# One matmul of a threshold guess later, the order in branch b's mixing, and other costs in a planner that interleaves a top-k search with dense work

## The chip, the cores and the metric

The kernel runs on one core of one Trainium2 chip. The metric is the device time of one execution in microseconds (us): 4260.66 before, the median of 3 runs from 4255.64 to 4262.76. Engines are written as in the profile: PE is TensorE's matmul, PEld its weight load, DVE is VectorE, ACT is ScalarE, POOL is GpSimd, SP is SyncE, which issues the DMAs.

## The reference

One encoder block over 4096 tokens of width 1024. Cut to what matters here:

```python
h = rms_norm(x, norm_g)
q, k, v, qi, ki, wi, z_a, u_b, z_b, gates = jnp.split(h @ w_in, SPLIT_POINTS, axis=-1)
# sparse attention, blocks of 128 queries: 8 index heads of 32 score all keys, the best 256 are kept
logits = jnp.einsum('bqhd,bsd->bqhs', qib, ki)
iscore = jnp.einsum('bqhs,bqh->bqs', jax.nn.relu(logits), wib)
iscore = jnp.where(allowed[None], iscore, -jnp.inf)      # allowed: by chunks of 64 tokens, not later
_, idx = lax.top_k(iscore, 256)                          # then softmax attention over these keys
a = dsa_attention(...) * silu(z_a)
# branch b, four groups of 128 channels, windows 2, 4, 8, 16: trailing mean minus the token, a 128x128 map
pooled = (c - lagged) / count - u_b
b = einsum('bsgc,gcd->bsgd', pooled, pool_w) * pool_scale * silu(z_b)
g = sigmoid(gates + merge_bias)
out = x + (g[0] * (a @ w_branch_a) + g[1] * (b @ w_branch_b)) @ w_out
```

## The kernel before

The kernel runs in stages. The first projects q, k, v and the index part and stores them in HBM, to about 445 us of the profile. The stage that the change touches, `phase_index`, runs from there to about 2100 us. Then a flag is checked (`phase_exact`, whose exact path is entered only where a threshold search did not settle), and attention and the output projections follow. Only the second stage's order differs between the two kernels.

In that stage two kinds of work lie beside each other:

- **Scoring and search.** For a block of 128 queries, each of 8 index heads and each piece of up to 1024 keys is one scoring tile, 624 in all: matmuls (L769) into one of 2 PSUM buffers `ps`, a Relu on ScalarE into one of 4 buffers `rl` (L772), and a multiply-accumulate on VectorE (L774) into an SBUF area of scores, `ring`. When a group of blocks is scored, its threshold is searched in 7 rounds: sign passes on ScalarE that count the scores above the threshold (L859), and small VectorE steps (L811 to L847); then the best are picked (`finish`).
- **Dense work.** The columns u, z_b, z_a and the gates of `h @ w_in`, in f32 made of three matmuls each (weight high · h high, weight high · h low, weight low · h high; L1056 to L1058). 24 matmuls make a unit of 128 columns x 256 tokens in one of 3 PSUM buffers `pd`; a unit is planned in `DU` = 4 quarters. A gate's unit is read out by a sigmoid (L1004, or L997 for z_a, which VectorE then multiplies, L999) and stored.

Branch b (`pool` in `dense`) takes the units of u and z_b, makes the windowed sums on GpSimd (L971), subtracts the token on VectorE (L980), rounds the result to its high part `ph` on ScalarE (L982), makes the low part `pl` on GpSimd (L983), and mixes channels by three matmuls through `mm3` (L347 high·`ph`, L348 high·`pl`, L349 low·`ph`). VectorE then scales and stores (L987).

The search starts from a guess of all thresholds (`guess`): a VectorE reduce and memset (L611, L612), a 128x1 matmul that sums over partitions (L639), a square root on ScalarE (L641), six VectorE steps (L615 to L620), another square root (L643) and some fifteen VectorE steps (L623 to L637). Its scratch lies at the end of `ring`. The second group's scores and every search wait for it.

The order on every engine is written by a planner before the program is built. Each step has an engine, a cost in us, a key (due time) and the steps it comes after. `Plan.run` is a list scheduler: at each time it gives a free engine the step with the lowest key whose inputs are done and whose buffers are free; a result reaches another engine `lat` later (here `LAT` = 0.1 us), a DMA's 2.0 us. On the chip each engine works its list strictly in order and waits at each instruction for its inputs, so a step that is listed too early blocks all behind it. The keys of scoring run from `t0[i]` to `t0[i+1]`, whose distance `span(i)` is `STR` times an estimate of the most loaded engine; those of dense units rise by 2.6 per unit; branch b's and the gates' read-outs are far ahead of all (`DEV`). Costs are constants in the code.

Of the kernel before, what the change touches and what calls it, by code (L numbers as in the profile page):

```python
# [12 lines left out]
F32 = mybir.dt.float32  # L13
# [4 lines left out]
AF = mybir.ActivationFunctionType  # L18
OP = mybir.AluOpType
# [4 lines left out]
S, D, P = 4096, 1024, 128  # L24
# [17 lines left out]
LAT = 0.1  # L42
# [28 lines left out]
DU = 4  # L71
# [11 lines left out]
CHN = 4.0  # L83
RING = 9984
T_IN = 10.0
STR = 0.8
PRL = 30.0
TKL = 30.0
DEV = 10000.0
# [157 lines left out]
class K:  # L247
# [338 lines left out]
    def guess(self, pl, new, ring, key):  # L586

        nc = self.nc
# [13 lines left out]
        ks, ones, c = take(1), take(P), take(1)  # L602
        a1, a2, a3 = take(*sh), take(*sh), take(*sh)
        mu, sd, sk, t = (take(NB) for _ in range(4))
# [3 lines left out]
        pc = new("pd")  # L608
# [27 lines left out]
            v.tensor_tensor(t, t, sd, op=OP.mult)  # L636
            v.tensor_tensor(self.SL, t, ch, op=OP.mult)  # L637
        s = pl.add("dve", 0.5, key, first, self.index_done)
        s = pl.add("pe", 0.1, key, lambda: nc.tensor.matmul(pc.t[:, 0:1], ones, ks, start=True, stop=True), [s], [pc])  # L639
        s = pl.add("dve", 0.2, key, lambda: v.tensor_copy(c, pc.t[:, 0:1]), [s], [pc])  # L640
        s = pl.add("act", 1.7, key, lambda: nc.scalar.activation(a1, self.qn2[:, :, 0:8], AF.Sqrt, scale=c), [s])  # L641
        s = pl.add("dve", 2.0, key, powers, [s])
# [3 lines left out]
    def phase_index(self):  # L646
# [13 lines left out]
        pl = Plan()  # L660
        new = pl.new
        w2 = 2 * P
# [81 lines left out]
        def scores(b, key, total, free):  # L744
# [6 lines left out]
            while os_:  # L751
# [8 lines left out]
                for h in range(8):  # L760
                    for o in some:
                        n = min(1024, L - o)
                        k_ = key(1)
                        ps, rl = new("ps"), new("rl")

                        def mm(ps=ps, o=o, n=n, h=h):
                            for s in range(0, n, 512):
                                e = min(n, s + 512)
                                pe.matmul(ps.t[:, s:e], t.t[:, h], self.kis[:, o + s:o + e], start=True, stop=True)  # L769
                        m = pl.add("pe", n * 0.42e-3, k_, mm, have + [base[o]] + ([s5] if o + n > S - P else []),  # L770
                                   use=[ps, t])
                        r = pl.add("act", 0.05 + n * 0.834e-3, k_, lambda ps=ps, rl=rl, n=n: act.activation(  # L772
                            rl.t[:, :n], ps.t[:, :n], AF.Relu), [m], use=[ps, rl])
                        prev[o] = pl.add("dve", 0.1 + n * 1.04e-3, k_, lambda rl=rl, o=o, n=n, h=h: v.scalar_tensor_tensor(  # L774
                            acc[:, o:o + n], rl.t[:, :n], self.wi[:, b, h:h + 1], acc[:, o:o + n], op0=OP.mult,
                            op1=OP.add), [r, prev[o], s2], use=[rl])
# [148 lines left out]
            ends.append(topk(i, t0[i + 1] - TKL, scored))  # L925

        self.dense(pl, new, rp)
        pl.run(LAT)
        es.close()
        self.esr.close()  # L930
        self.phase_exact()
# [2 lines left out]
    def dense(self, pl, new, rp):  # L934
# [19 lines left out]
        def pool(c, g, t, pu, pz, done):  # L954
# [11 lines left out]
            def sums():  # L966
# [6 lines left out]
                if c == 0:  # L973
# [5 lines left out]
            ph, pq, pm = new("ph"), new("pl"), new("pd")  # L979
            s = pl.add("dve", 0.4, k, lambda: v.scalar_tensor_tensor(  # L980
                cur.t[:, 16:], cur.t[:, 16:], 1.0 / win, u.t[:, 16:], op0=OP.mult, op1=OP.subtract), [s], use=[cur, u])
            s = pl.add("act", 0.31, k, lambda: act.activation(ph.t, cur.t[:, 16:], AF.Copy), [s], use=[cur, ph])  # L982
            s = pl.add("pool", 0.69, k, lambda: po.tensor_tensor(pq.t, cur.t[:, 16:], ph.t.bitcast(F32), op=OP.subtract),  # L983
                       [s], use=[cur, ph, pq])
            s = pl.add("pe", 0.33, k, lambda: self.mm3(pm.t[:, :w2], lambda k: wm[g][0], lambda k: wm[g][1],
                                                       lambda k: ph.t, lambda k: pq.t, 1), [s], use=[ph, pq, pm])
            s = pl.add("dve", 0.4, k, lambda: v.scalar_tensor_tensor(  # L987
                zs.t, pm.t[:, :w2], self.col[:, 24 + g:25 + g], zs.t, op0=OP.mult, op1=OP.mult), [s, m], use=[pm, zs])
            pl.add("dma", 0.4, k, lambda: dma(self.bD[g, :, c * w2:(c + 1) * w2], zs.t), [s], use=[zs])
# [41 lines left out]
        for s, mine in enumerate(sweeps):  # L1031
# [3 lines left out]
            for c in range(S // w2):  # L1035
# [12 lines left out]
                for m, (kind, i) in enumerate(mine):  # L1048
                    pd = new("pd")
                    wh, wl, have = W[s, m]  # L1050
                    for half in range(DU):
                        def mm(half=half, pd=pd, wh=wh, wl=wl, H=H):
                            out = pd.t[:, :w2].rearrange("p (r n) -> p r n", n=P)
                            for k in range(KT // DU * half, KT // DU * (half + 1)):
# [1 line left out]
                                pe.matmul(out, wh.t[:, k], r1, start=(k == 0), stop=False)  # L1056
                                pe.matmul(out, wh.t[:, k], r2, start=False, stop=False)  # L1057
                                pe.matmul(out, wl.t[:, k], r1, start=False, stop=(k == KT - 1))  # L1058
                        prev = pl.add("pe", 2.58 / DU, t, mm, lds + [have, prev], use=[pd, wh, wl] + H)
                        t += unit / DU  # L1060
                    if kind == "u":
                        pu = (pd, prev)
# [586 lines left out]
```

## Time and profile before

| | us |
|---|---|
| median of 3 runs | 4260.66 (4255.64 to 4262.76) |
| the profiled execution | 4263.0 |
| its span, first to last instruction | 4261.2 |
| PE busy | 4142.3 (97%) |
| DVE busy | 3218.5 (76%) |
| ACT busy | 2340.6 (55%) |
| POOL busy | 1900.7 (45%) |

The span is 1.8 us shorter than the time of the same execution. The mean granted TensorE clock is 0.986 of full speed. A wait is read as "engine, line <- who ended it": the idle time of the engine just before that line's instruction. A window gives the busy time of each engine in a stretch. Times of the stretches count from the span's start.

### The profile page before, as it was taken

The page shows a single profiled execution, that of the slowest core. Times are in us where ns is not written, and L with a number is a line of the kernel's source. Part 1 is how long each engine was busy: PE and PEld are TensorE (multiplying, and loading weights), DVE is VectorE, ACT ScalarE, POOL GpSimd, SP SyncE. Part 2 cuts the span into 40 slices and gives each one's busy share as a digit, 9 for nine tenths or more (in the row PEclk, how much of TensorE's full clock was granted, in tenths as well). Part 3 has the DMA queues.
Part 4 walks back from the last instruction along what each step waited for, and adds up shares of the span by engine and source line. Part 5 has one row for each costly group of instructions (what it writes and reads, how often), then busy time and mean ns, then how long its engine had stood idle before and what let it go on. Part 6 is the DMA issues. An engine that isn't in the chain of part 4 may idle for free.

```text
span 4261.2 us, 76795 instructions
## 1 busy us (share of the span) xinstructions
PE 4142.3 (97%) x27746; PEld 3496.7 (82%) x27747; DVE 3218.5 (76%) x7786; ACT 2340.6 (55%) x3977; POOL 1900.7 (45%) x1717
## 2 busy tenths in 40 slices
PE   8999899999999999999799999999999999999999
PEld 7888899899999998999756666666666658999998
DVE  6555688889889888788679999999999995434342
ACT  4444588777877877887455555555555552111110
POOL 3445322323234333010047888888999991111110
PEclk9999999999999999999889999999999999999999
DMA  6666644545445446566543212212111116544442
GB/s 225 236 243 231 218 160 167 172 172 187 162 174 168 160 170 196 201 234 206 184 84 72 58 45 49 47 48 52 43 41 38 23 42 190 163 134 151 137 144 77
DMA packets 446651, 586.34 MB, mean 138 GB/s; under 512 B 149373, under 2 KB 342457, under 8 KB 442042
## 3 DMA queue, kind: packets, MB, share of 16 engines
q1 hardware_dynamic: 446266, 581.39, 41.9%
q8 instruction: 219, 3.59, 0.3%
q14 instruction: 166, 1.36, 0.1%
HBM read 388.54 MB, written 175.54 MB: 132 GB/s over the span
## 4 chain that ended last, share of the span: by engine, by line
PE 57%; DVE 2%; DMA 1%; issue 1%; ACT 0%; POOL 0%; SPq 0%; DVEq 0%; ACTq 0%; POOLq 0%
PE pv L1339 11%; PE st L1323 7%; PE ps L1284 6%; PE st L1324 5%; PE pd L1056 3%; PE pd L1057 3%; PE pd L1058 3%; PE po L1537 3%; PE po L1538 3%; PE po L1539 3%; PE pa L1538 3%; PE pa L1539 3%; PE pa L1537 3%; PE ps L769 1%; PE st L1375 1%; PE st L341 1%
## 5 line engine op out<-in xcount | busy, mean ns | idle before, releaser
L1056 PE MATMUL pd<-h,wgh 128*128 128x256 f32 x3584 | 1018.6, 284 | 1.3 <-DVE zsm L976 1.3
L1057 PE MATMUL pd<-h,wgh 128*128 128x256 f32 x3584 | 1012.0, 282 | 0.0
L1058 PE MATMUL pd<-h,wgl 128*128 128x256 f32 x3584 | 1011.4, 282 | 0.0
L1354 POOL TENSOR_TENSOR acc<-acc,tt 128x1024 f32<-128x1024 f32 x388 | 927.5, 2391 | 103.0 <-ACT tt L1330 80.7
L1330 ACT ACTIVATE tt<-tt 128x512 f32<-128x512 f32 x1056 | 652.7, 631 | 556.0 <-DVE tt L1327 553.9
L1327 DVE TENSOR_TENSOR tt<-st,bT 128x512 f32<-128x512 f32 x1056 | 693.6, 684 | 76.4 <-PE st L1324 59.3
L774 DVE SCALAR_TENSOR_TENSOR ring<-rl,wi,ring 128x1024 f32<-128x1024 f32 (+7 forms) x624 | 689.8, 1148 | 12.9 <-ACT rl L772 10.3
L1056 PEld LDWEIGHTS pd<-h,wgh 128*128 128x128 f32 x3584 | 680.3, 190 | 19.6 <-issue 1.5
L1057 PEld LDWEIGHTS pd<-h,wgh 128*128 128x128 f32 x3584 | 681.2, 190 | 14.6
L1290 DVE CUSTOM_DVE_ANT_0 jk<-ps,bias 128x1024 bf16<-128x1024 f32 (+7 forms) x640 | 656.2, 1029 | 47.2 <-PE ps L1284 46.0
L1058 PEld LDWEIGHTS pd<-h,wgl 128*128 128x128 f32 x3584 | 681.4, 190 | 0.0
L772 ACT ACTIVATE rl<-ps 128x1024 f32<-128x1024 f32 (+7 forms) x624 | 539.0, 889 | 133.8 <-PE ps L769 61.4
L1339 PE MATMUL pv<-tt,vv 128*64 128x256 f32 x4224 | 525.0, 389 | 0.0
L859 ACT ACTIVATE sg<-ring,tk 128x2048 fp8e4<-128x2048 f32 (+7 forms) x322 | 485.4, 1509 | 38.3 <-DVE tk L846 21.2
L1323 PE MATMUL st<-qa,kk 128*128 128x512 f32 x1056 | 453.2, 429 | 10.5 <-ACT sm L1379 5.5
L1339 PEld LDWEIGHTS pv<-tt,vv 128*64 128x64 f32 x4224 | 279.6, 137 | 210.3 <-issue 71.6
L1324 PE MATMUL st<-qm,kl 65*128 65x512 f32 x1056 | 420.9, 399 | 2.3 <-DMA qm<-maxD 2.3
L1579 POOL TENSOR_TENSOR ga<-ga,gb 128x256 f32<-128x256 f32 x128 | 100.3, 792 | 617.4 <-DVE ga L1574 504.2
L1284 PE MATMUL ps<-kk,qa 128*128 128x512 f32 (+3 forms) x1152 | 362.2, 390 | 0.7 <-DVE mx L1290 0.7
L769 PE MATMUL ps<-kis,qT 128*128 128x512 f32 (+3 forms) x1136 | 334.9, 382 | 14.7 <-ACT rl L772 14.4
L1502 ACT ACTIVATE yh<-ga 128x256 fp32r<-128x256 f32 x128 | 53.3, 418 | 500.7 <-PE po L1538 297.8
L1323 PEld LDWEIGHTS st<-qa,kk 128*128 128x128 f32 x1056 | 200.1, 190 | 153.5 <-DVE tt L1327 49.2
(331 smaller groups left out, 7801.9 us busy)
## 6 DMA issues: line engine op xcount, KB each, us to landing
h<-hD SPq DMA_DIRECT2D x192, 1024.0 KB
hlD<-rhl SPq DMA_DIRECT2D x32, 1216.0 KB
gD<-sgm SPq DMA_DIRECT2D x256, 128.0 KB
x<-x SPq DMA_DIRECT2D x32, 512.0 KB
wraw<-w_in SPq DMA_DIRECT2D x32, 512.0 KB
hD<-hh SPq DMA_DIRECT2D x32, 512.0 KB
hD<-hl SPq DMA_DIRECT2D x32, 512.0 KB
q<-hlD SPq DMA_DIRECT2D x32, 512.0 KB
```

The costliest lines, as they stand in the source:

```text
L774: prev[o] = pl.add("dve", 0.1 + n * 1.04e-3, k_, lambda rl=rl, o=o, n=n, h=h: v.scalar_tensor_tensor(acc[:, o:o + n], rl.t[:, :n], self.wi ...
L1056: pe.matmul(out, wh.t[:, k], r1, start=(k == 0), stop=False)
L1057: pe.matmul(out, wh.t[:, k], r2, start=False, stop=False)
L1058: pe.matmul(out, wl.t[:, k], r1, start=False, stop=(k == KT - 1))
L1284: pe.matmul(ps.t[:, s:e], Q[b][0].t[:, 4 * g + j], kk[:, g, o + s:o + e], start=True, stop=True)
L1290: v.tensor_tensor_reduce(out=jk.t[:, :n], in0=ps.t[:, :n], in1=BI[b][0].t[:, o:o + n], scale=1.0, scalar=-3e38, op0=OP.add, op1=OP.max, ac ...
L1323: pe.matmul(s.t, kk[:, g, o], qa.t[:, hs], start=True, stop=False)
L1324: pe.matmul(s.t, kl[:, g, o], qm.t[:, hs], start=False, stop=True)
L1327: ad = pl.add("dve", 0.602, i, lambda s=s, tt=tt, r=r, kt=kt: v.tensor_tensor(tt.t[:, r], s.t, bc(bt.t[:, kt:kt + 1], [P, 4, P]), op=OP.ad ...
L1330: E[kt] = pl.add("act", 0.52, i, lambda tt=tt, r=r: act.activation(tt.t[:, r], tt.t[:, r], AF.Exp), [ad], use=[tt])
L1339: pe.matmul(pv.t[64 * f:64 * f + 64], vv[:, k, 64 * g:64 * g + 64], T[k // 2].t[:, k % 2, 2 * f:2 * f + 2], start=(k == 0), stop=(k == b))
L1354: gp.tensor_tensor(acc.t, first, tt.t, op=OP.add)
```

## The change

Two due times and several costs change, a matmul's place in the plan, and the order of three matmuls:

- `STR`, which stretches the due times of scoring, goes from 0.8 to 0.85.
- The guess's 128x1 matmul gets the key 25 instead of -40.
- The planner's cost of scoring matmuls goes from 0.42 to 0.45 ns an element, of a dense unit from 2.58 to 2.86 us, of branch b's rounding from 0.31 to 0.42, its low part from 0.69 to 1.0, its mixing from 0.33 to 0.36, and `run` gets twice the latency, 0.2 us.
- Branch b's mixing runs high·`ph`, low·`ph`, high·`pl`, so that the low part `pl` is read by the third matmul instead of the second.

```diff
--- before.py
+++ after.py
@@ -83,7 +83,7 @@
 CHN = 4.0
 RING = 9984
 T_IN = 10.0
-STR = 0.8
+STR = 0.85
 PRL = 30.0
 TKL = 30.0
 DEV = 10000.0
@@ -636,7 +636,7 @@
             v.tensor_tensor(t, t, sd, op=OP.mult)
             v.tensor_tensor(self.SL, t, ch, op=OP.mult)
         s = pl.add("dve", 0.5, key, first, self.index_done)
-        s = pl.add("pe", 0.1, key, lambda: nc.tensor.matmul(pc.t[:, 0:1], ones, ks, start=True, stop=True), [s], [pc])
+        s = pl.add("pe", 0.1, 25, lambda: nc.tensor.matmul(pc.t[:, 0:1], ones, ks, start=True, stop=True), [s], [pc])
         s = pl.add("dve", 0.2, key, lambda: v.tensor_copy(c, pc.t[:, 0:1]), [s], [pc])
         s = pl.add("act", 1.7, key, lambda: nc.scalar.activation(a1, self.qn2[:, :, 0:8], AF.Sqrt, scale=c), [s])
         s = pl.add("dve", 2.0, key, powers, [s])
@@ -767,7 +767,7 @@
                             for s in range(0, n, 512):
                                 e = min(n, s + 512)
                                 pe.matmul(ps.t[:, s:e], t.t[:, h], self.kis[:, o + s:o + e], start=True, stop=True)
-                        m = pl.add("pe", n * 0.42e-3, k_, mm, have + [base[o]] + ([s5] if o + n > S - P else []),
+                        m = pl.add("pe", n * 0.45e-3, k_, mm, have + [base[o]] + ([s5] if o + n > S - P else []),
                                    use=[ps, t])
                         r = pl.add("act", 0.05 + n * 0.834e-3, k_, lambda ps=ps, rl=rl, n=n: act.activation(
                             rl.t[:, :n], ps.t[:, :n], AF.Relu), [m], use=[ps, rl])
@@ -925,7 +925,7 @@
             ends.append(topk(i, t0[i + 1] - TKL, scored))
 
         self.dense(pl, new, rp)
-        pl.run(LAT)
+        pl.run(2 * LAT)
         es.close()
         self.esr.close()
         self.phase_exact()
@@ -979,11 +979,14 @@
             ph, pq, pm = new("ph"), new("pl"), new("pd")
             s = pl.add("dve", 0.4, k, lambda: v.scalar_tensor_tensor(
                 cur.t[:, 16:], cur.t[:, 16:], 1.0 / win, u.t[:, 16:], op0=OP.mult, op1=OP.subtract), [s], use=[cur, u])
-            s = pl.add("act", 0.31, k, lambda: act.activation(ph.t, cur.t[:, 16:], AF.Copy), [s], use=[cur, ph])
-            s = pl.add("pool", 0.69, k, lambda: po.tensor_tensor(pq.t, cur.t[:, 16:], ph.t.bitcast(F32), op=OP.subtract),
+            s = pl.add("act", 0.42, k, lambda: act.activation(ph.t, cur.t[:, 16:], AF.Copy), [s], use=[cur, ph])
+            s = pl.add("pool", 1.0, k, lambda: po.tensor_tensor(pq.t, cur.t[:, 16:], ph.t.bitcast(F32), op=OP.subtract),
                        [s], use=[cur, ph, pq])
-            s = pl.add("pe", 0.33, k, lambda: self.mm3(pm.t[:, :w2], lambda k: wm[g][0], lambda k: wm[g][1],
-                                                       lambda k: ph.t, lambda k: pq.t, 1), [s], use=[ph, pq, pm])
+
+            def mix():
+                for i, (x, y) in enumerate(((0, ph), (1, ph), (0, pq))):
+                    pe.matmul(pm.t[:, :w2], wm[g][x], y.t, start=(i == 0), stop=(i == 2))
+            s = pl.add("pe", 0.36, k, mix, [s], use=[ph, pq, pm])
             s = pl.add("dve", 0.4, k, lambda: v.scalar_tensor_tensor(
                 zs.t, pm.t[:, :w2], self.col[:, 24 + g:25 + g], zs.t, op0=OP.mult, op1=OP.mult), [s, m], use=[pm, zs])
             pl.add("dma", 0.4, k, lambda: dma(self.bD[g, :, c * w2:(c + 1) * w2], zs.t), [s], use=[zs])
@@ -1056,7 +1059,7 @@
                                 pe.matmul(out, wh.t[:, k], r1, start=(k == 0), stop=False)
                                 pe.matmul(out, wh.t[:, k], r2, start=False, stop=False)
                                 pe.matmul(out, wl.t[:, k], r1, start=False, stop=(k == KT - 1))
-                        prev = pl.add("pe", 2.58 / DU, t, mm, lds + [have, prev], use=[pd, wh, wl] + H)
+                        prev = pl.add("pe", 2.86 / DU, t, mm, lds + [have, prev], use=[pd, wh, wl] + H)
                         t += unit / DU
                     if kind == "u":
                         pu = (pd, prev)
```

No tile, buffer count or shape changes. From about L986 on a line of the kernel before has a number 3 higher in the changed one (dense matmuls L1059 to L1061, z_a's sigmoid L1000, gates L1007); the mixing matmuls stand in L988.

The planned order moves at many places; three are shown. On TensorE, at the stage's start, the kernel before has these rows (`pd` is the dense unit's PSUM tile or the guess's, `pt` the PSUM tile of the transposes of `qi`, the index queries of a block):

```order
L1056 MATMUL pd_5395<-h_5020,wgh_5032 128x256
L1057 MATMUL pd_5395<-h_5022,wgh_5032 128x256
L1058 MATMUL pd_5395<-h_5020,wgl_5033 128x256
L639 MATMUL pd_5420<-ring 128x1
L341 MATMUL pt_5422<-identr,qi_5384 128x128 x4
L1056 MATMUL pd_5395<-h_5020,wgh_5032 128x256
L1057 MATMUL pd_5395<-h_5022,wgh_5032 128x256
L1058 MATMUL pd_5395<-h_5020,wgl_5033 128x256
L1056 MATMUL pd_5395<-h_5020,wgh_5032 128x256
```

And the changed kernel, at the same place:

```order
L1059 MATMUL pd_5396<-h_5020,wgh_5032 128x256
L1060 MATMUL pd_5396<-h_5022,wgh_5032 128x256
L1061 MATMUL pd_5396<-h_5020,wgl_5033 128x256
L341 MATMUL pt_5420<-identr,qi_5384 128x128 x4
L1059 MATMUL pd_5396<-h_5020,wgh_5032 128x256
L1060 MATMUL pd_5396<-h_5022,wgh_5032 128x256
L1061 MATMUL pd_5396<-h_5020,wgl_5033 128x256
L1059 MATMUL pd_5396<-h_5020,wgh_5032 128x256
```

The guess's matmul is gone from here, and the transposes of `qi` come right behind the dense matmuls; it now stands 217 rows later, between two quarters of a dense unit.

On ScalarE, around the guess, the kernel before has (`u` and `sgm` are branch b's and the gates' read-outs, `ring` the guess's scratch; ACT_TABLE_LOAD loads a function table):

```order
L641 ACTIVATE ring<-qn_75,ring 128x256
L961 ACTIVATE u_5361<-pd_5363 128x256
L962 ACT_TABLE_LOAD
L962 ACTIVATE sgm_5464<-pd_5395 128x256
L740 ACTIVATE qT_5423<-pt_5437 128x512
L1004 ACTIVATE sgm_5491<-pd_5445,col 128x256
L643 ACT_TABLE_LOAD
L643 ACTIVATE ring<-ring 128x32
L982 ACTIVATE ph_5531<-s_5480 128x256
L1004 ACT_TABLE_LOAD
L1004 ACTIVATE sgm_5550<-pd_5484,col 128x256
```

The changed kernel, whose first table load in the stage comes earlier, under L962, has there:

```order
L772 ACTIVATE rl_5793<-ps_5783 128x1024
L772 ACTIVATE rl_5805<-ps_5795 128x1024
L641 ACT_TABLE_LOAD
L641 ACTIVATE ring<-qn_75,ring 128x256
L1007 ACT_TABLE_LOAD
L1007 ACTIVATE sgm_5839<-pd_5773,col 128x256
L772 ACTIVATE rl_5847<-ps_5819 128x1024
L772 ACTIVATE rl_5861<-ps_5830 128x1024
L643 ACT_TABLE_LOAD
L643 ACTIVATE ring<-ring 128x32
L772 ACTIVATE rl_5874<-ps_5866 128x1024
L772 ACTIVATE rl_5898<-ps_5870 128x1024
```

The two square roots now stand among the scoring's Relus (L772) and each is followed by a sigmoid with its own table load: five loads in the stage instead of three.

ScalarE's last rows of the stage, before (`sg` is a sign pass over `ring`, `tk` the thresholds; L997 is the sigmoid of a z_a unit):

```order
L997 ACTIVATE sgm_27851<-pd_27779 128x256
L859 ACTIVATE sg_27874,tk_26462<-ring,tk_26462 128x384
L997 ACTIVATE sgm_27884<-pd_27843 128x256
L859 ACTIVATE sg_27892,tk_26462<-ring,tk_26462 128x512
L997 ACTIVATE sgm_27944<-pd_27876 128x256
L859 ACTIVATE sg_27960,tk_26462<-ring,tk_26462 128x384
L859 ACTIVATE sg_27969,tk_26462<-ring,tk_26462 128x512
L997 ACTIVATE sgm_27971<-pd_27937 128x256
L859 ACTIVATE sg_28003,tk_26462<-ring,tk_26462 128x384
L859 ACTIVATE sg_28006,tk_26462<-ring,tk_26462 128x512
L859 ACTIVATE sg_28034,tk_26462<-ring,tk_26462 128x384
L859 ACTIVATE sg_28042,tk_26462<-ring,tk_26462 128x512
```

In the changed kernel, the last sign pass and what comes behind it:

```order
L859 ACTIVATE sg_27320,tk_25572<-ring,tk_25572 128x384
L1000 ACTIVATE sgm_27329<-pd_27291 128x256
L859 ACTIVATE sg_27360,tk_25572<-ring,tk_25572 128x512
L1000 ACTIVATE sgm_27375<-pd_27322 128x256
L1000 ACTIVATE sgm_27421<-pd_27368 128x256
L1000 ACTIVATE sgm_27456<-pd_27408 128x256
L1000 ACTIVATE sgm_27485<-pd_27447 128x256
L1000 ACTIVATE sgm_27517<-pd_27478 128x256
```

Behind its last sign pass stand 23 read-outs of z_a units, the last rows of the stage on ScalarE; in the kernel before the search's sign passes come last.

On TensorE, a mixing of branch b, before:

```order
L1057 MATMUL pd_6018<-h_5685,wgh_5168 128x256
L1058 MATMUL pd_6018<-h_5630,wgl_5169 128x256
L347 MATMUL pd_6028<-ph_6008,wm0h 128x256
L348 MATMUL pd_6028<-pl_6015,wm0h 128x256
L349 MATMUL pd_6028<-ph_6008,wm0l 128x256
L769 MATMUL ps_6032<-kis,qT_5423 128x512 x2
L1056 MATMUL pd_6018<-h_5630,wgh_5168 128x256
L1057 MATMUL pd_6018<-h_5685,wgh_5168 128x256
```

And in the changed kernel:

```order
L1060 MATMUL pd_6038<-h_5622,wgh_5322 128x256
L1061 MATMUL pd_6038<-h_5567,wgl_5323 128x256
L988 MATMUL pd_6048<-ph_6002,wm0h 128x256
L988 MATMUL pd_6048<-ph_6002,wm0l 128x256
L988 MATMUL pd_6048<-pl_6029,wm0h 128x256
L769 MATMUL ps_6055<-kis,qT_5421 128x512 x2
L1059 MATMUL pd_6038<-h_5567,wgh_5322 128x256
L1060 MATMUL pd_6038<-h_5622,wgh_5322 128x256
```

The low part `pl` is read by the third of the three. In the order as a whole, 9948 of the stage's 10752 dense matmuls stand ahead of the 601st scoring tile before and 9300 in the changed kernel.

## Rows read from the trace of the kernel before

**Rows 1.** Page, part 1: busy us of each engine (share of the span) xinstructions
```profile
PE 4142.3 (97%) x27746; PEld 3496.7 (82%) x27747; DVE 3218.5 (76%) x7786; ACT 2340.6 (55%) x3977; POOL 1900.7 (45%) x1717
```

**Rows 2.** Waits of PE, 440 to 2101 us: us in total, times, longest
```profile
PE ps L769 <- ACT rl L772: 14.4, 10, 4.3
PE pd L639 <- DVE ring L612: 14.2, 1, 14.2
PE pc L1078 <- DVE one L1076: 12.7, 1, 12.7
PE pd L348 <- POOL pl L983: 11.2, 17, 1.3
PE pd L347 <- ACT ph L982: 2.2, 3, 1.6
PE pd L347 <- ACT sgm L1004: 1.4, 1, 1.4
```

**Rows 3.** Windows: us, busy of PE, PEld, DVE, ACT, POOL (x), clock, DMA
```profile
490.00:1988.00 1498.00, 1466.15 (x11292) 1408.47 (x11291) 1282.40 (x3787) 1166.38 (x1697) 385.02 (x441) 1.00 0.52 179
583.00:710.00 127.00, 127.00 (x986) 122.81 (x985) 109.56 (x283) 93.30 (x128) 28.81 (x36) 1.00 0.48 173
847.00:1030.00 183.00, 181.60 (x1409) 175.30 (x1408) 160.53 (x503) 138.61 (x203) 45.50 (x59) 1.00 0.46 163
1030.00:1103.00 73.00, 68.27 (x520) 64.41 (x520) 66.47 (x215) 57.52 (x82) 33.18 (x33) 1.00 0.59 197
1225.00:1376.00 151.00, 145.33 (x1111) 139.19 (x1111) 138.49 (x460) 112.92 (x168) 60.65 (x67) 0.99 0.51 176
2030.00:2088.00 58.00, 57.49 (x484) 57.28 (x482) 41.41 (x226) 28.68 (x65) 0.00 (x0) 1.00 0.60 211
```

**Rows 4.** Timeline of PE, 449 to 466 us: start, duration, [idle before <-releaser]
```profile
449.87 0.28 PE L1058 MATMUL pd<-h,wgl 128*128 128x256 f32 x1
464.31 0.56 PE L639 MATMUL pd<-ring 128*128 128x1 f32 x2 [14.16 <-DVE ring L612]
465.20 0.72 PE L341 MATMUL pt<-identr,qi 128*128 128x128 f32 x4 [0.33 <-DMA qi<-hlD]
```

**Rows 5.** Timeline of SyncE's queue, 457 to 463 us
```profile
461.56 0.38 SPq L729 DMA_DIRECT2D qi<-hlD  x1
```

**Rows 6.** Lines of ACT, 460 to 480 us: busy, mean ns | idle before
```profile
L643 ACT ACT_TABLE_LOAD x1 | 1.3, 1283 | 0.0
```

**Rows 7.** Windows of the guess's two VectorE blocks, columns as in rows 3
```profile
466.99:469.64 2.65, 2.65 (x15) 2.65 (x15) 2.58 (x7) 2.39 (x4) 1.29 (x3) 0.50 1.02 416
474.43:479.24 4.81, 4.81 (x40) 4.56 (x39) 4.33 (x16) 3.87 (x6) 3.54 (x4) 1.00 0.96 286
```

**Rows 8.** Line 983 on POOL: ns min/median/max, and who waited (us, times)
```profile
L983 POOL TENSOR_TENSOR pl<-s,ph x64: 721/1008/1874, 474.8 to 1645.2; 128x256 fp32r<-128x256 f32 x64
  PE pd L348: 11.2, 17
```

**Rows 9.** Waits of PE in 1030:1103 (first two), then 1225:1376 us
```profile
PE ps L769 <- ACT rl L772: 1.6, 2, 1.4
PE pd L1056 <- DVE zsm L976: 1.3, 1, 1.3
PE ps L769 <- ACT rl L772: 1.8, 2, 1.6
```

**Rows 10.** Timelines of PE, ACT and DVE, 2087 to 2101 us
```profile
2087.21 0.28 PE L1058 MATMUL pd<-h,wgl 128*128 128x256 f32 x1
2100.15 0.27 PE L1078 MATMUL pc<-flag,one 128*1 128x32 f32 x2 [12.66 <-DVE one L1076]
2087.52 0.38 ACT L997 ACTIVATE sgm<-pd 128x256 f32<-128x256 f32 x1 [0.25 <-PE pd L1058]
2090.08 0.42 DVE L999 TENSOR_TENSOR zsm<-pd,sgm 128x256 f32<-128x256 f32 x1
```

## The prediction

> **What bounds the kernel now.** I read the engine table first. TensorE is busy 97% of a 4261.2 us span [rows 1], so the kernel gets shorter only where TensorE idles; an engine that gets faster beside it gives nothing. The profiled execution took 4263.0 us (span plus 1.8 us around it), 2.3 us above the median of the runs, 4260.66. I add up against 4263.0 and take the 2.3 off at the end.
>
> The change touches only the plan of the search phase, about 440 to 2101 us. Next I read the waits of TensorE in it [rows 2]: 14.2 us in one piece at the start (threshold guess), 12.7 us in one piece at the end (flag count), 14.4 us in 10 waits for a free scoring PSUM buffer, and 11.2 + 2.2 + 1.4 us in the mixing matmuls of branch b. About 57 us is all that a plan can win here; the matmul work stays what it was.
>
> Then windows, for how much room the other engines have. Up to 1988 us, where all but some 20 of the 624 scoring tiles are through, VectorE is busy 1282.40 of 1498 us, 85.6% [rows 3]. Where TensorE never waits, VectorE is at 86.3% (109.56 of 127). In the two densest stretches it is at 91.5% (66.47 + 138.49 of 224) and TensorE loses 10.4 of 224 us. So VectorE is the next limit, and close.
>
> **A. The start (key of the guess's matmul).** The guess's matmul L639 keeps TensorE idle for 14.16 us, from the end of a dense matmul at 450 to 464.3 [rows 4]. The new order puts it 217 rows later, and the first thing behind the dense matmuls is then the transposes L341 of qi. In the same rows these wait for qi's DMA until 465.20, and SyncE issues that load only at 461.56 [rows 5]; its queue has the same order as before. So this stall gets a new owner: TensorE resumes at 465.2 minus at most the matmul's 0.56. Gain 0 to 0.6.
> What the later guess adds: the square roots L641 and L643 now stand singly among sigmoids, so ScalarE loads its table five times around the guess instead of three, 2 x 1283 ns [rows 6], amid the scoring tiles instead of beside an idle TensorE. VectorE's two blocks of the guess, 2.65 and 4.81 us [rows 7], also fall between accumulations (L774). Two PSUM buffers and four rl buffers cover part. Bounds of the whole term: -0.6, and +5 (the longer block in full). I take +1, near the covered end, because TensorE ran through the second block before without a loss (busy 4.81 of 4.81, VectorE 4.33) [rows 7].
>
> **B. Branch b's mixing.** Each mixing is three matmuls; the middle one, L348, takes the low part that GpSimd makes. It waits visibly 17 of 64 times, 11.2 us in all, mean 0.66, longest 1.3 [rows 2]. L983 takes 1.008 us at the median [rows 8] where the old plan charged 0.69. In the new plan the mixing comes later by 0.11 (ScalarE's cost) + 0.31 (GpSimd's) + 3 x 0.1 (crossings between engines) = 0.72 us, and the low part's matmul has one more matmul ahead of it, 57.49/484 = 0.119 us each [rows 3]: 0.84 in all. That covers all waits below 0.84, and what is left of the longest is 0.5. I take -9 of 11.2, and -2 of the 3.6 us of L347, whose producer ScalarE also gets 0.11 + 0.2 more: -11. Bounds 0 and -14.8.
> L983 runs from 721 over 1008 to 1874 ns for one shape [rows 8], so something slows it at times. The Trainium skill, "GPSIMD Engine Reference", section "1. Specifications", says that GpSimd shares its SBUF interfaces with VectorE and contends with VectorE's instructions of two SBUF inputs; L774 is of that kind. By that rule a fuller VectorE would stretch L983 towards 1.87, 0.87 more than the median, which cancels the 0.84: B would be 0 and the sum -1 instead of -12. The spread agrees with the rule but no row here names the cause.
>
> **C. The balance of scoring and dense work.** The new costs (2.86 for a dense unit, .45 for scoring) are near the rows: a unit of 24 matmuls is 24 x 0.119 = 2.85. But with STR and the latency they also change the mix. Counted in the written-out order, 9948 dense matmuls stand ahead of scoring tile 601 before and 9300 after: 648 fewer, 648 x 0.119 = 77 us less TensorE work beside the same VectorE work. The window of 1498 us becomes 1421, and VectorE's share 1282.4/1421 = 90.2%, between the stretches without waits (86.3%) and those at 91.5%. In the latter, waits other than the mixing's are 1.6 + 1.3 + 1.8 = 4.7 of 224 us, 2.1% [rows 9]. Charged for all 1421 us that is 30; on the line from 0% at 86.3% to 2.1% at 91.5% the share of 90.2% gives 1.6%, 22. Before it was 14.4 + 1.3 in the same windows. So +7 to +14; I take +9. Bounds: -15.7 (none left), and +41 (the worse stretch, 2.9 of 73, for all 1421).
>
> **D. The end.** Before, the last dense matmul ends at 2087.5, and TensorE then waits 12.66 us for the search's last rounds and the memset before the flag matmul [rows 10]. In the new ScalarE order the last sign pass (L859) stands 22 gates ahead of the last gate: dense work is last by about 22 x 2.85 = 63 us. What then follows the last dense matmul is a sigmoid (0.38), its product (0.42) in front of the memset on VectorE, and the crossings, some 1.3 us in all. 12.66 - 1.3 = -11.3. Bounds -12.4 and, if the search runs late by the whole 63 us, 0; I take -11.3: the search now lags the dense work by 12.66 and would have to slip by five times that.
>
> Sum: +1 - 11 + 9 - 11.3 = -12.3, so 4263.0 - 12.3 = 4250.7, and 4248 in terms of the median.
>
> **Rivals.**
> 1. *All visible waits but the start go.* The measured costs place scoring so well that C turns to -15.7 while B gives 13 and D 12: about -41, 4220. For it: a stretch at 87.7% VectorE (160.53 of 183) lost only 1.4 us. Against: 90.2% is above any stretch that ran without waits.
> 2. *No change.* The low part stretches with VectorE's load (B = 0), or the mixing's waits only move to the other matmuls, since the mixing keeps its own PSUM buffer: +1 + 0 + 9 - 11.3 = -1, about 4259. For it: L983's longest 1874 ns. Against: the visible waits are short, and 0.84 is more than their mean.
> 3. *Slower: VectorE sets the pace of scoring.* Place: PSUM to rl to L774, until tile 601. If VectorE can hold only 88%, near what it holds where TensorE is full, instead of 90.2%, the window is 1282.4/0.88 = 1457 instead of 1421: 36 us of new idle time, with the tail regained, B's waits hidden in it: 36 + 1 - 11.3 = +26, 4286. It decides from 1282.4/(1421 + 10) = 89.6% downwards, only half a per cent below what the forecast needs. For it: the share needed is near the highest seen, and sustained for 1400 us. Against: 91.5% was held over 224 us with TensorE at 95%.
> 4. *The change doesn't do what it says at the start*: that is in the forecast already (A).
> ScalarE's table: the Trainium skill, "ScalarE: Activation LUTs", section "Table sets: the hidden batching unit", says that alternating functions of different sets pays a load each time, about 2.7 us in its example. The rows give 1.283 and the measurement decides; by the page the two extra loads would be 5.4 us, and A at most +3 higher.
>
> **How the numbers follow.** A measurement of this kernel tells 0.2%, 8.5 us, from no change. Forecast 42%, its own range 4236 to 4262 (C from -2 to +20); rival 1 14%; rival 2 24%; rival 3 20%. Faster: 0.42 x 0.8 + 0.14 + 0.24 x 0.2 = 0.52. Same: 0.42 x 0.2 + 0.24 x 0.7 + 0.20 x 0.1 = 0.27. Slower: 0.21, the rest. The range reaches half of rival 1 and the milder half of rival 3: 4226 to 4278.
>
> **What would show it right or wrong.** A: TensorE's waits list a stall of about 14 us at the start under L341 and qi's DMA, none under L639, and five table loads. B: waits of the mixing matmuls on GpSimd's low part of at most 2 us, and L983's median still about 1.0; a median of 1.3 or more makes rival 2 right. C: waits of L769 on ScalarE between 15 and 35 us, and VectorE at about 90% up to where scoring tile 601 ends (about 1910); above 45 us of them rival 3 holds, none of them is rival 1. D: the flag matmul waits under 2 us, and the last sign pass ends 50 us or more ahead of it. The forecast falls if the sum of TensorE's waits in this phase is not between 33 and 60 us.

## The result and the profile after

The changed kernel takes 4299.27 us (median of 6 runs, 4297.51 to 4303.25) against 4262.07 of the kernel before in the same runs (6 runs). The ratio is 1.0089, 95% interval [1.0079, 1.0099]: it is slower by 37 us, where 12 us faster was forecast. The profiled execution has a span of 4301.1 us against 4261.2. TensorE is still busy 97% of it, and the busy time itself has grown by 22 us (4142.3 in [rows 1]). Part 1 of the page, with the columns of [rows 1]:

```profile
PE 4164.4 (97%) x27746; PEld 3507.8 (82%) x27747; DVE 3211.0 (75%) x7786; ACT 2340.1 (54%) x3979; POOL 1914.7 (45%) x1717
```

The flag matmul, which ends the stage, starts at 2140.41 instead of 2100.15. So all of the 39.9 us of span (40.3) are lost inside the stage. TensorE's waits in it, to be laid beside [rows 2]:

```profile
PE ps L769 <- ACT rl L772: 32.3, 43, 4.2
PE pt L341 <- DMA qi<-hlD: 15.1, 1, 15.1
PE pd L988 <- POOL pl L983: 14.9, 18, 1.8
PE pt L341 <- ACT qT L740: 5.9, 4, 3.2
PE pd L1059 <- DVE zsm L976: 2.1, 1, 2.1
PE pd L988 <- ACT ph L982: 2.1, 2, 1.1
PE pd L988 <- ACT sgm L1007: 1.4, 1, 1.4
PE pc L1081 <- DVE one L1079: 1.0, 1, 1.0
```

Two of these are as forecast. The guess's 14.2 us went to `qi`'s load (15.1), and the flag's 12.7 fell to 1.0. But the scoring waits rose from 14.4 to 32.3 us, in 43 pieces instead of 10. The mixing did not fall either: 14.9 + 2.1 + 1.4 = 18.4 us instead of 11.2 + 2.2 + 1.4 = 14.8. No term of the forecast had the 5.9 us in four transposes that wait for ScalarE's `qT` (before 0.5). The listed waits sum to 74.8, before (with three small ones that [rows 2] leaves out) to 58.2: 16.6 of the 40.3 us. The others lie in time in which TensorE counts as busy, as windows show (columns as in [rows 3]; 490 to 1962 reaches to scoring tile 601, as 490 to 1988 did before):

```profile
490.00:1962.00 1472.00, 1412.40 (x10638) 1344.09 (x10637) 1271.63 (x3798) 1159.08 (x1675) 403.05 (x447) 0.99 0.49 170
1060.00:1065.00 5.00, 2.57 (x18) 1.97 (x18) 4.90 (x14) 3.13 (x5) 3.98 (x3) 1.00 0.37 107
1065.00:1070.00 5.00, 5.00 (x29) 4.92 (x29) 3.66 (x19) 2.96 (x3) 0.59 (x2) 0.66 0.50 157
1080.00:1085.00 5.00, 2.16 (x8) 1.97 (x9) 2.91 (x5) 4.97 (x8) 3.03 (x5) 0.75 0.42 101
1085.00:1090.00 5.00, 5.00 (x37) 4.82 (x37) 4.80 (x5) 2.21 (x5) 3.02 (x3) 0.91 0.09 30
```

Up to tile 601 TensorE ran 654 instructions fewer than before (10638, 11292 in [rows 3]). At 0.119 us each its busy time should be 1466.15 - 77.8 = 1388; it is 1412.40, 24 us more. The two pairs of short windows show where some of that comes from. From 1060 to 1065 TensorE is busy for 2.57 of 5 us, because three waits (0.97, 0.32 and 1.15 us) stand close together; from 1080 to 1085 it is busy for 2.16, because of one wait of 3.84 us. Right behind the first its granted clock is 0.66; in and behind the second it is 0.75 and 0.91: mixes of the two levels, 1.2 and 2.4 GHz. Added up over the windows of 10 us from 490 to 2080, the clock's shortfall is 18.7 us of full speed after and 5.1 before. So waits that are long or stand close together cost TensorE more than the list of waits shows. The rest of the 24 us stays open.

VectorE's share up to tile 601 is 1271.63/1472 = 86.4%, before 85.6%; the forecast had 90.2%.

Start and tail, TensorE's timeline, and the last sign pass on ScalarE (to be compared with [rows 4, 10]):

```profile
465.99 0.72 PE L341 MATMUL pt<-identr,qi 128*128 128x128 f32 x4 [15.12 <-DMA qi<-hlD]
```

```profile
2139.08 0.28 PE L1061 MATMUL pd<-h,wgl 128*128 128x256 f32 x1
2140.41 0.22 PE L1081 MATMUL pc<-flag,one 128*1 128x32 f32 x2 [1.05 <-DVE one L1079]
```

```profile
2075.11 0.72 ACT L859 ACTIVATE sg<-ring,tk 128x512 fp8e4<-128x512 f32 x1 [1.02 <-DVE rl L887]
```

TensorE goes on at 466 with the transposes of `qi`, as it did at 464.3 with the guess's matmul before. At the end dense work is last by 64 us, and the flag matmul follows after 1.05. The table loads on ScalarE, five, as [rows 6] but more of them:

```profile
L962 ACT ACT_TABLE_LOAD x2 | 2.6, 1283 | 0.0
L641 ACT ACT_TABLE_LOAD x1 | 1.3, 1283 | 0.0
L1007 ACT ACT_TABLE_LOAD x1 | 1.3, 1283 | 0.0
L643 ACT ACT_TABLE_LOAD x1 | 1.3, 1283 | 0.0
```

### The profile page after: what moved, and what is told of

Read it like the earlier page. It is cut to its first block, busy times and chain, and to the rows that moved or that the text cites. A ratio compares the mean times of both kernels' runs of the same rounds, so it can differ in the third digit from the quotient of the medians.

```text
span 4301.1 us, 76801 instructions
## 1 busy us (share of the span) xinstructions
PE 4164.4 (97%) x27746; PEld 3507.8 (82%) x27747; DVE 3211.0 (75%) x7786; ACT 2340.1 (54%) x3979; POOL 1914.7 (45%) x1717
## 4 chain that ended last, share of the span: by engine, by line
PE 46%; DMA 1%; DVE 1%; POOL 1%; issue 1%; SPq 0%; ACT 0%; DVEq 0%; POOLq 0%; ACTq 0%
PE pv L1342 11%; PE st L1326 7%; PE ps L1287 6%; PE st L1327 5%; PE po L1540 3%; PE po L1541 3%; PE po L1542 3%; PE pa L1541 3%; PE pa L1542 3%; PE pa L1540 3%; PE st L1378 1%; PE st L341 1%; POOL acc L1357 0%; DVE tt L1330 0%; DMA maxD<-mf 0%
## 5 line engine op out<-in xcount | busy, mean ns | idle before, releaser
L1059 PE MATMUL pd<-h,wgh 128*128 128x256 f32 x3584 | 1020.8, 285 | 2.1 <-DVE zsm L976 2.1
L1061 PE MATMUL pd<-h,wgl 128*128 128x256 f32 x3584 | 1014.3, 283 | 0.0
L774 DVE SCALAR_TENSOR_TENSOR ring<-rl,wi,ring 128x1024 f32<-128x1024 f32 (+7 forms) x624 | 693.4, 1153 | 18.4 <-ACT rl L772 16.0
L1059 PEld LDWEIGHTS pd<-h,wgh 128*128 128x128 f32 x3584 | 682.8, 191 | 22.4 <-DVE zsm L976 2.3
L1293 DVE CUSTOM_DVE_ANT_0 jk<-ps,bias 128x1024 bf16<-128x1024 f32 (+7 forms) x640 | 656.7, 1030 | 45.1 <-PE ps L1287 35.0
L1061 PEld LDWEIGHTS pd<-h,wgl 128*128 128x128 f32 x3584 | 683.6, 191 | 0.0
L772 ACT ACTIVATE rl<-ps 128x1024 f32<-128x1024 f32 (+7 forms) x624 | 539.1, 890 | 194.4 <-DVE ring L774 65.0
L859 ACT ACTIVATE sg<-ring,tk 128x2048 fp8e4<-128x2048 f32 (+10 forms) x322 | 485.5, 1509 | 59.3 <-DVE tk L846 37.2
L769 PE MATMUL ps<-kis,qT 128*128 128x512 f32 (+3 forms) x1136 | 353.6, 392 | 32.9 <-ACT rl L772 32.3
```

The lines of the kernel that those rows point to most:

```text
L1293: v.tensor_tensor_reduce(out=jk.t[:, :n], in0=ps.t[:, :n], in1=BI[b][0].t[:, o:o + n], scale=1.0, scalar=-3e38, op0=OP.add, op1=OP.max, ac ...
```

## The experiments

**Theories.** Theory 1, formed from this trace: the planner's cost of a dense unit does it. In its first form (called balance, later 1b) only the amount of dense work beside the scoring counts. In the form 1a, the old undercharge of TensorE (2.58 planned, 2.85 on the chip) was a slack: each unit took 0.27 us longer than planned, so the other engines, whose costs are too low as well, had their results ready. With TensorE alone charged in full that slack is gone. Theory 2: the later guess, or latency and mixing. Each experiment's interval is that of its ratio to the kernel before, run beside it.

### 1 to 4: which part does it

e1, the kernel before with the dense cost alone:

```diff
-prev = pl.add("pe", 2.58 / DU, t, mm, lds + [have, prev], use=[pd, wh, wl] + H)
+prev = pl.add("pe", 2.86 / DU, t, mm, lds + [have, prev], use=[pd, wh, wl] + H)
```

> The kernel before with one edit: the planner charges a dense unit 2.86 us instead of 2.58. 8952 dense matmuls then stand ahead of scoring tile 601 (9948 before, 9300 in the change). Theory 1 (balance: VectorE holds only some 86% whatever the plan wants, so a plan that puts less dense work beside the scoring leaves TensorE idle and dense work to the end): slower than the whole change, 4325 to 4350 us; VectorE's share up to tile 601 stays at 85 to 88%, the flag matmul waits under 2 us. Theory 2 (the guess, later and with more table loads amid scoring, delays everything): 4250 to 4270, since the guess stands as before.

Measured: 4316.22 us, 1.0125 [1.0108, 1.0141]. The one constant makes the kernel slower than the whole change does, though less than expected (4325 at least). VectorE's share up to tile 601 is 87.0% (1256.80 of 1444 us), within the expected 85 to 88%. TensorE's waits in the stage:

```profile
PE ps L769 <- ACT rl L772: 34.1, 35, 3.4
PE pd L348 <- POOL pl L983: 27.8, 35, 2.0
PE pd L347 <- ACT ph L982: 6.6, 6, 3.3
```

The mixing waits, 14.8 us before, are 34 (27.8 + 6.6); a theory that has the balance of scoring and dense work alone gives no reason for that.

e2, the changed kernel with this line undone (`2.58 / DU`):

> The changed kernel with the old cost of a dense unit, 2.58 us; all else as changed. 9948 dense matmuls stand ahead of tile 601, as before. Theory 1 (balance): 4252 to 4266 us, the scoring waits back to about 15 us and the tail's wait back to about 10. Theory 2 (guess, or latency and mixing): 4285 to 4300.

Measured: 4256.44 us, 0.9989 [0.9979, 0.9998]. All the loss is gone, with guess, latency, `STR` and mixing as changed.

```profile
PE ps L769 <- ACT rl L772: 20.6, 20, 4.4
PE pd L988 <- POOL pl L983: 2.5, 5, 1.2
PE pc L1081 <- DVE one L1079: 14.0, 1, 14.0
```

With TensorE undercharged the new mixing waits 2.5 us on the low part, as term B had it. Theory 2 falls.

e3, the changed kernel with the guess's key back at -40:

```diff
-s = pl.add("pe", 0.1, 25, lambda: nc.tensor.matmul(pc.t[:, 0:1], ones, ks, start=True, stop=True), [s], [pc])
+s = pl.add("pe", 0.1, key, lambda: nc.tensor.matmul(pc.t[:, 0:1], ones, ks, start=True, stop=True), [s], [pc])
```

> The changed kernel with the guess's matmul key back at -40; all else as changed, 9300 dense matmuls ahead of tile 601 as in the change. Theory 1 (balance): 4294 to 4302 us, the stall at the start back under the guess's matmul. Theory 2 (guess): under 4275.

Measured: 4296.2 us, 1.0084 [1.0068, 1.0101], as theory 1 had it and not to be told from the change. The guess's place is worth a few us at most.

e4, the changed kernel with `STR = 0.90`:

> The changed kernel with STR 0.90 instead of 0.85: scoring is due later, 9810 dense matmuls ahead of tile 601, and the dense work ends about where the search ends. Theory 1 (balance): 4245 to 4262 us, scoring waits of TensorE 12 to 22 us. Theory 2 (guess, or latency and mixing): 4285 or more, since nothing of the guess differs from the change.

Measured: 4280.32 us, 1.0045 [1.0029, 1.0062]: a miss. The balance is nearly that of before, and still 20 us are lost.

```profile
PE ps L769 <- ACT rl L772: 22.4, 24, 2.7
PE pd L988 <- POOL pl L983: 13.0, 17, 1.5
PE pd L988 <- ACT ph L982: 8.6, 4, 3.4
```

The scoring waits are near those of e2 (20.6) and the tail's wait is 1.4 us, but the mixing still costs 21.6 us, and the clock's shortfall from 490 to 2080 is 17.0 us, nearly that of the change. So the balance alone (1b) does not explain the loss; 1a was formed here.

### 5 to 8: slack, the other engines' costs, VectorE's load, the dose

e5, the changed kernel with branch b charged too much:

```diff
-s = pl.add("act", 0.42, k, lambda: act.activation(ph.t, cur.t[:, 16:], AF.Copy), [s], use=[cur, ph])
-s = pl.add("pool", 1.0, k, lambda: po.tensor_tensor(pq.t, ...
+s = pl.add("act", 0.8, k, lambda: act.activation(ph.t, cur.t[:, 16:], AF.Copy), [s], use=[cur, ph])
+s = pl.add("pool", 2.5, k, lambda: po.tensor_tensor(pq.t, ...
```

> The changed kernel, whose planner charges branch b's rounding 0.8 us (0.42) and its low part 2.5 us (1.0), far more than they take; 9324 dense matmuls ahead of scoring tile 601 (9300 in the change). Theory 1a (with TensorE charged in full the hand-offs lost the slack that the undercharged dense unit gave them): TensorE's waits in the mixing fall from 18 us to under 5, the scoring waits stay at 28 to 40, time 4280 to 4290. Theory 1b (only the balance of scoring and dense work counts, and what is won at the mixing comes back as scoring waits): 4295 to 4303.

Measured: 4277.96 us, 1.0037 [1.0023, 1.0051], 2 us below what 1a had: about 21 us of the 37 come back, though the balance is as in the change.

```profile
PE ps L769 <- ACT rl L772: 33.4, 42, 3.3
PE pd L988 <- ACT sgm L1007: 0.7, 1, 0.7
```

The mixing's wait on the low part is off the list; the scoring waits stay.

e6, the changed kernel with the other engines' costs raised towards what the trace shows:

```diff
-prev[o] = pl.add("dve", 0.1 + n * 1.04e-3, ...
+prev[o] = pl.add("dve", 0.1 + n * 1.15e-3, ...
-pieces.append(pl.add("dve", 0.3 + n * 2.08e-3, ...
+pieces.append(pl.add("dve", 0.3 + n * 2.17e-3, ...
-s = pl.add("dve", 0.08 + n * 0.52e-3, ...
+s = pl.add("dve", 0.08 + n * 0.70e-3, ...
-s = chain[g] = pl.add("pool", 0.2 + 0.69 * (g + 1), ...
+s = chain[g] = pl.add("pool", 0.5 + 0.85 * (g + 1), ...
-e0 = pl.add("pool", 0.17, ...
+e0 = pl.add("pool", 0.8, ...
-e1 = pl.add("act", 0.62, ...
+e1 = pl.add("act", 0.74, ...
```

> The changed kernel with the other engines' costs raised to what the trace shows too (L774 0.1 + 1.15 ns an element, the picking of the best 2.17, the bias 0.70, branch b's sums 0.5 + 0.85 a step, halo 0.8, its read-out 0.74); 9498 dense matmuls ahead of tile 601. Theory 1a (the plan failed because it charges TensorE in full and the others too little): mixing waits under 6 us, scoring waits under 22, time 4255 to 4270. Theory 1b (balance alone): between the change and the kernel without the dense cost by the count, 4299 - 43 x 198/648 = about 4286. Theory 3 (mean costs do not help, since single instructions vary and a plan without slack waits anyway): 4290 to 4300.

Measured: 4266.47 us, 1.001 [1.0001, 1.002]. TensorE is charged in full, and 33 of the 37 us are back; the count alone would have given 4286. The waits, and the window up to tile 601:

```profile
PE ps L769 <- ACT rl L772: 19.8, 27, 3.2
PE pd L988 <- POOL pl L983: 4.7, 8, 1.0
PE pd L988 <- ACT sgm L1007: 3.0, 2, 1.6
```

```profile
490.00:1949.00 1459.00, 1423.70 (x10837) 1359.18 (x10836) 1275.67 (x3806) 1157.58 (x1682) 385.15 (x447) 0.99 0.51 175
```

The scoring waits are back at those of e2 (20.6). The mixing waits are 7.7 us, more than the 6 expected and than e2's 3.1, but far from the change's 18.4. So it was not the full charge of TensorE as such, but that charge beside too low ones. Of what is left, 10 us over e2, about half is the clock's shortfall (10.2 us for 5.1 in e2); the rest is not explained.

e7, the changed kernel with half of VectorE's accumulate:

```diff
-acc[:, o:o + n], rl.t[:, :n], self.wi[:, b, h:h + 1], acc[:, o:o + n], op0=OP.mult,
+acc[:, o:o + n // 2], rl.t[:, :n // 2], self.wi[:, b, h:h + 1], acc[:, o:o + n // 2], op0=OP.mult,
-nc.vector.memset(one, 1.0)
+nc.vector.memset(one, 0.0)
```

> The changed kernel in the same order, but the accumulate on VectorE (L774) works on half of each tile's columns, so half of the scores are left out, and the flag's ones are zeros, so that the exact path is not entered. VectorE has some 340 us less work. Theory 1 (VectorE cannot keep the pace that the plan asks of it): the scoring waits of TensorE fall from 32 us to under 10, the mixing waits to under 8, time 4240 to 4262. Rival (the waits come from the alternation of sign passes and small steps, or from ScalarE, not from VectorE's load): scoring waits stay above 22, time above 4280.

Measured: 4245.79 us, 0.9963 [0.9949, 0.9977]. The time is as expected, the scoring waits only in part. The waits, and the window up to tile 601 (columns as in [rows 3]):

```profile
PE ps L769 <- ACT rl L772: 18.5, 24, 3.8
PE pd L988 <- ACT sgm L1007: 1.4, 1, 1.4
PE pd L988 <- POOL pl L983: 0.6, 2, 0.5
```

```profile
490.00:1910.00 1420.00, 1393.63 (x10638) 1333.64 (x10637) 991.85 (x3805) 1153.73 (x1677) 339.87 (x447) 0.99 0.51 176
```

In the same order as the change, with 991.85 us of VectorE's work instead of 1271.63, tile 601 comes 52 us earlier (1910 for 1962), the mixing waits go from 18.4 to 2.0 and 14 us of the scoring waits go. So VectorE's load decides, in two ways that this run does not separate: VectorE itself comes late (branch b's chain runs through it too, L980), and GpSimd's low part L983 takes 0.88 us in the mean instead of 1.15, since fewer of them are stretched beside L774 (25 of 64 take over 0.8 us, 39 in the change; more under B below). The scoring waits were to fall under 10 and stay at 18.5 us with half of the accumulate; before there were 14.4 with all of it.

e8, the changed kernel with `2.65 / DU`:

> The changed kernel with a dense unit charged 2.65 us, between 2.58 and 2.86; 9780 dense matmuls ahead of tile 601 (9948 with 2.58, 9300 with 2.86), and 4 gates behind the last sign pass. Theory 1 (dose by the count): 4256 + 43 x 168/648 = about 4267, less up to 12 for the tail's wait that goes: 4256 to 4268, mixing waits 4 to 9 us. Were it only a matter of the full charge, with a step at 2.86: within 3 us of 4256.

Measured: 4250.3 us, 0.9976 [0.9966, 0.9985]: faster than both kernels, and below both expectations.

```profile
PE ps L769 <- ACT rl L772: 20.9, 24, 3.2
PE pd L988 <- POOL pl L983: 6.3, 9, 1.5
PE pc L1081 <- DVE one L1079: 1.0, 1, 1.0
```

The scoring waits are as in e2, the mixing waits (9.1 us with two smaller lines of 1.4) between, and the tail's wait of 14.0 is gone. The tail's part of the forecast (D) pays once dense work is last by little. e4 has nearly the same count ahead of tile 601 (9810), with 2.86 for a unit and scoring due later, and takes 30 us more: the charge tells, and not the count alone.

### 9 to 12: the terms by themselves

e9, the kernel before with branch b's part alone (its costs and the order of its three matmuls, as in the diff of the change):

> The kernel before with branch b's part alone: the order of the three mixing matmuls and the costs 0.42, 1.0 and 0.36. 9900 dense matmuls ahead of tile 601 (9948 before). The forecast's term B priced by itself: with TensorE undercharged as before, the mixing waits fall from 14.8 us to under 4, time 4250 to 4256. Rival (what the mixing wins comes back as scoring waits): 4257 to 4264.

Measured: 4257.06 us, 0.9992 [0.9983, 1.0001]: at the lower end of the rival's range, above that of term B, and not told apart from no change.

```profile
PE ps L769 <- ACT rl L772: 15.2, 14, 4.3
PE pd L988 <- POOL pl L983: 6.0, 10, 1.7
PE pd L988 <- ACT ph L982: 1.6, 3, 0.7
```

The mixing waits fall from 14.8 to 7.6 us, about two thirds of term B, where TensorE stays undercharged (under 4 us expected). They did not come back as scoring waits, as the rival had it: these are 15.2 us for 14.4.

e10, e8 with a first load charged later:

```diff
-s0 = pl.add("dma", 0.8, -50, lambda: dma(r31, self.rowD[rows, 0:296]))
+s0 = pl.add("dma", 8.0, -50, lambda: dma(r31, self.rowD[rows, 0:296]))
```

> The kernel of e8 (dense unit 2.65) with one more cost: the planner charges the stage's first load 8.0 us instead of 0.8, so the transposes of qi are listed behind some 70 more dense matmuls at the stage's start. If the stall at the start is only the wait for qi's load (the forecast's term A), it shrinks from 15.4 us to 6 to 8 and the time is 4241 to 4246. Rival (TensorE then waits at the same time for the next block of h or a free PSUM buffer): the stall keeps 12 us or more under another line, time 4248 to 4254.

Measured: 4248.02 us, 0.997 [0.9958, 0.9981], not told apart from e8. TensorE's timeline:

```profile
461.28 0.58 PE L1059 MATMUL pd<-h,wgh 128*128 128x256 f32 x1 [8.96 <-ACT u L961]
467.81 0.45 PE L341 MATMUL pt<-identr,qi 128*128 128x128 f32 x4
```

The transposes now come without a wait, but TensorE stops 8.96 us for a PSUM buffer that ScalarE has not read out: the start passes from one owner to the next. The stall lies between the two expectations and the time at the lower end of the rival's. It is 6.4 us shorter than in e8, but the flag matmul comes only 3.1 us earlier (2085.8 for 2088.9), with scoring waits of 23.8 us for 20.9.

e11, the changed kernel with a planner that hands results to TensorE later:

```diff
-d.ready = max(d.ready, now + (2.0 if s.eng == "dma" else lat if d.eng != s.eng else 0.0))
+d.ready = max(d.ready, now + (2.0 if s.eng == "dma" else lat + (1.0 if d.eng == "pe" else 0.0) if d.eng != s.eng else 0.0))
```

> The changed kernel with all its costs, but the planner lets every result that another engine hands to TensorE arrive 1.0 us later than to others (1.2 us instead of 0.2). 9324 dense matmuls ahead of tile 601 (9300 in the change). Theory 1a (the full charge of TensorE took away a slack, and any slack in the hand-offs to it restores that part): the mixing waits fall from 18 us to under 5; the scoring waits, which are for a buffer that ScalarE frees and so get no such slack, stay at 27 to 37; time 4274 to 4286. Theory 1b (it was the costs of branch b's steps as such, or the balance): mixing waits 12 us or more, time 4293 to 4303.

Measured: 4283.47 us, 1.0051 [1.0036, 1.0066]. This line is in the planner that the two later stages share, so these changed too: from the flag matmul to the end the span has 4282.5 - 2110.1 = 2172.4 us, where the change has 4301.1 - 2140.4 = 2160.7. In the stage itself, read at the flag matmul, 30 us of the 40 come back (2110.1 for 2140.4), by slack alone, with every cost as changed. The mixing waits fall as 1a had it, the scoring waits a little more (27 at least expected). The waits, and the window up to tile 601:

```profile
PE ps L769 <- ACT rl L772: 25.8, 42, 3.8
PE pd L988 <- POOL pl L983: 2.7, 5, 1.3
```

```profile
490.00:1935.00 1445.00, 1407.09 (x10670) 1340.44 (x10669) 1266.12 (x3800) 1158.21 (x1679) 405.31 (x447) 0.99 0.51 174
```

e12, e8 with the same line:

> The kernel of e8 (dense unit 2.65) with the same 1.0 us of slack into TensorE; 9798 dense matmuls ahead of tile 601 (9780 in e8). Theory 1a: the mixing waits fall from 9 us to under 3, scoring waits stay near 20, time 4241 to 4248. Theory 1b: 4248 to 4256.

Measured: 4262.89 us, 1.0006 [0.9997, 1.0015], missing both expectations for the same reason: the stage ends at 2088.3 (e8 2088.9) and the later stages take 13 us longer (2173 for 2160).

```profile
PE ps L769 <- ACT rl L772: 25.6, 31, 4.2
PE pd L988 <- ACT sgm L1007: 2.0, 1, 2.0
PE pd L988 <- POOL pl L983: 0.2, 1, 0.2
```

The mixing waits, 9.1 us in e8, are 2.2, but the scoring waits rose by 4.7: with little to win, the slack comes back in another list.

## Why the prediction was wrong

**C is the step that failed.** "The window of 1498 us becomes 1421, and VectorE's share 1282.4/1421 = 90.2%": it became 1472, at 86.4%. The working priced what happens at 90% from two stretches of the old kernel (224 us at 91.5%), in which TensorE still took 11% longer for a unit than its plan said. That lag kept the others ahead. The change removed the lag, and the same share could then not be held: e7 shows that VectorE's load decides, e6 that charging it (and GpSimd and ScalarE) near what they take brings the pace back, e5 and e11 that slack alone brings most of it. The term was put at +9 with an end at +41. With B's gain the window was to be about 1421 - 11 + 9 = 1419 us. Against 1421 the measured one is 51 us longer: TensorE is idle in it for 28 us more (59.6 for 31.9, the mixing's 3.6 included), and busy for 24 us more than its matmuls account for, 13.6 of them by the clock. One marker for C was poor as well: the scoring waits (32.3) lay inside the 15 to 35 that was to speak for the forecast. VectorE's share and the sum of the waits (74.8, outside 33 to 60) did speak against it. The prediction's first reading, that an engine that gets faster beside TensorE gives nothing, falls with C: in e7 VectorE's shorter work alone gives 53 us.

**B failed for the same reason.** The 0.84 us by which the low part's matmul comes later were worked out in the plan's time with TensorE's lag taken as unchanged. They were right where it was (2.5 us of waits on the low part in e2). In the change they were eaten up, and the waits are 18.4, not about 4. L983 itself hardly changed: its median is 1040 ns, 1008 before, its mean 1.15 us, 1.14 before.

```profile
L983 POOL TENSOR_TENSOR pl<-s,ph x64: 721/1040/1851, 470.6 to 1699.6; 128x256 fp32r<-128x256 f32 x64
```

So the rival that GpSimd slows (a median of 1.3) did not happen either. What stretches single ones the trace does show, though. Of the 64 in the change 39 take more than 0.8 us, and every one of these runs beside L774 or L887, which read two tensors in SBUF; of the 25 shorter ones three do. 14 of the 18 waits on the low part follow one of 1.2 us or more, as here:

```profile
1575.51 4.14 DVE L774 SCALAR_TENSOR_TENSOR ring<-rl,wi,ring 128x1024 f32<-128x1024 f32 x3
1576.80 1.76 POOL L983 TENSOR_TENSOR pl<-s,ph 128x256 fp32r<-128x256 f32 x1
1578.62 0.39 PE L988 MATMUL pd<-pl,wm3h 128*128 128x256 f32 x1 [1.53 <-POOL pl L983]
```

At 1025.28 one took 0.72 us, with VectorE idle. The Trainium skill ("GPSIMD Engine Reference", section "1. Specifications") names this contention of GpSimd with VectorE's instructions of two SBUF inputs. The traces agree with it, but there was no more of it than before, when 38 of the 64 took over 0.8 us: it is part of why the mixing waits at all, not of why it waits longer.

**A and D held.** The stall passed to `qi`'s load, as worked out, with five table loads; the transposes came at 465.99 instead of at 465.20 at the latest, and e3 prices the guess's move at nothing that can be told. The flag's wait fell by 11.6 us (11.3 forecast), with the last sign pass 64 us ahead. But D's gain can only be had once, and being ahead by 63 us went with a scoring drawn further forward than that gain needs: e8 has the same tail with 4 read-outs behind the last sign pass.

**The rivals.** Rival 3 named the outcome: VectorE sets the pace until tile 601. It was given 20%, at 88% and +26 us; by its own formula at 86.4% it would be 1484 - 1421 + 1 - 11.3 = +53, measured +37. Its mechanism was half of it: VectorE is not at a limit of its own at 86.4%, since e6 and e11 run the same work up to tile 601 at 87.4 and 87.6% (1275.67 of 1459 and 1266.12 of 1445). What the plan lacked was slack in the lists. And no rival had the clock: 13.6 us of full speed more were lost to it than before.

What stays open: why e6 is still some 10 us slower than e2 and 16 slower than e8 (the clock is 5 and 7 of them), what the slack of each hand-off was (it was inferred from e5, e6 and e11, not read from the traces), and where the 18.5 us of scoring waits that remain with half of the accumulate come from.

## What to carry to other kernels

In an order written from a table of costs, look at the costs' ratio between engines; here it decided: an undercharge of the bottleneck engine is a slack for all who feed it, and correcting it alone takes that away, so correct the feeders in the same step or keep the slack on purpose. Price a new density not by stretches of the old schedule at that density, but ask what kept them calm. And where waits are long or stand close together, add what the clock loses behind them to the sum of the waits.

## What was not expected of the hardware

TensorE's granted clock fell to a mix of its two levels (0.66 over 5 us) right behind 5 us in which it was busy for 2.57, in the middle of a stage that runs at 1.00 for most of its time; summed up, such falls cost 18.7 us of full speed in the change, 3.4 in e8 and 5.1 before. GpSimd's 128x256 subtraction takes some 0.74 us (the median in e7 740 ns, in e6 746), or up to 1.85 in the change beside VectorE's accumulate, so its median jumps between kernels that differ only in order (849 in e5, 1120 in e8). The accumulate is stretched too: over 1024 columns it takes 1.28 us at the median and at most 1.29 where no GpSimd instruction runs beside it (268 in the change), and up to 3.11 where one does (148).
